# Two layers of two blocks on one core: the eight feature tiles of u_hi 1088 bytes apart instead of 1024

## The chip, the core and the metric

One Trainium2 chip, one of its cores. The metric is the device time of one execution in microseconds (us). Engine names: PE is TensorE (PEld its weight load), DVE is VectorE, ACT is ScalarE, POOL is GpSimd, SP issues the loads. "The stationary operand" is the one that a weight load puts into the array before a matmul, "the moving operand" the one that the matmul then streams through.

## What is computed

The reference runs two blocks of two layers over x [256 tokens, 1024 features]. The first block's layers are an attention (differential in layer 0, neighbourhood in layer 1), a SwiGLU feed-forward of width 2816 and a gated per-layer embedding. The second block's layers are a mixer (gated convolution and pooling in layer 0; a forgetting attention and a block attention in layer 1) and a convolutional feed-forward of width 2816. A root-mean-square norm stands ahead of each. Cut to what matters here:

```python
hn = rmsnorm(h, norm_mix[i]);  h = h + attention(hn)          # q, k, v and output products, 1024 wide
h = h + (silu(hn @ w_gate) * (hn @ w_up)) @ w_down             # 1024 -> 2 x 2816 -> 1024
h = h + sigmoid(hn @ ple_w_gate) * (p[i] @ ple_w_proj)         # 1024 -> 1024
h = h + (silu(conv(z[..., :2816])) * z[..., 2816:]) @ w_out    # second block's feed-forward
```

All arrays are float32. Nearly all the work is products of a [256, K] activation with a weight matrix that is read once from HBM.

## The kernel before

Activations lie with features on the 128 partitions: eight feature tiles (KT = 8) of 256 tokens (S = 256). A float32 product is made of three float32r matmuls: each operand is split exactly into a high and a low part, and the product is hi*hi + hi*lo + lo*hi (`mm3`, L198). Every matmul is issued at L195 by `mm`, so all products share that line in the profile and are told apart by their tiles.

`Weights` (L53 to L104) reads the weight chunks of 128 x 1024 float32 (4096 bytes on each partition) in the order in which PE takes them: SP loads a chunk into one of five `stage` buffers (L71), ACT writes `w_hi` (L88), DVE writes `w_lo` (L89), eight buffers of each. A block of 128 x 128 weights is a slice of 512 bytes on each partition.

The moving operand of a product is one of these:

- `u_hi`, `u_lo` (`split_act`, L221): the operand of eight feature tiles, two buffers each. ACT writes u_hi (L256, L572, L616, L885, L898), DVE u_lo (L258, L573, L617 and others). They are read by the input products `out_tile` into `ps_g` (all q, k, gate, up and in-products) and by the output products of the attentions and of the even mixer into `acc`. In the v-products (`ps_v`, `pz`) the parts change places: slices of u are stationary, and the weights move.
- `m` (L724): the high and the low part of one feed-forward tile, side by side in one tile of 2048 bytes, the moving operand of the down-products into `acc`. `pool_m` is built in the same way.
- `p_part`: the split embedding inputs, the high and the low part in two tiles, moving operands of `ps_p`.

For one pair of weight block and feature tile the order is: w_hi stationary with u_hi moving, w_hi again with u_lo, w_lo with u_hi. Each matmul has a weight load of its own, and the load for the next matmul runs while a matmul streams.

The tile pools place their buffers one behind the other in SBUF. The starts on a partition in the built program, and what each leaves over when divided by 512 (a weight block's length):

| tile | start before | left over | start after | left over |
|---|---|---|---|---|
| w_hi, w_lo (8 + 8 buffers) | 53216 + 4096 i | 480 | the same | 480 |
| u_hi, first buffer, tile k | 118752 + 1024 k | 480 | 118752 + 1088 k | 480 + 64 k |
| u_hi, second buffer, tile k | 126944 + 1024 k | 480 | 127392 + 1088 k | 416 + 64 k |
| u_lo, both buffers | 135136 + 1024 k | 480 | 136032 + 1024 k | 352 |
| p_part | 184288 | 480 | 185184 | 352 |
| m, pool_m | 192544 | 32 | 193440 | 416 |

So "the offset" of a moving operand to the weight blocks, the difference of the two remainders (counted round 512), was 0 for u_hi, u_lo and p_part and 64 for m. In the text a negative offset means that the moving operand's start lies below the weight block's in this count.

Of the kernel before, what the change touches and what calls it, by code (L numbers as in the profile page):

```python
# [11 lines left out]
F32R = mybir.dt.float32r  # L12
# [8 lines left out]
FF = 2816  # L21
FT = FF // 128
NEG = -1.0e30
FLOOR = -3.0e38
# [7 lines left out]

# After how many steps of the products around them the parts of an attention are issued.
LAG = {"da": (2, 8, 11, 14), "da_every": 3, "pair": (2, 5, 7), "every": 2}
# [16 lines left out]


class Weights:  # L53
    """The weights in the order in which TensorE takes them: loaded ahead, each split
    exactly into two float32r parts (w = hi + lo). A chunk with a destination is split
    into tiles that it makes."""

# [49 lines left out]
def network(ctx: ExitStack, tc: tile.TileContext, x_t, p_t, cols, b_v, na_bias, t5_bias, w_mats, out):  # L107
# [9 lines left out]

# [1 line left out]
    chunks = []  # L119
# [40 lines left out]

# [1 line left out]
    h = const.tile([128, KT, S], F32, name="h")  # L162
# [6 lines left out]

# [1 line left out]
    off = const.tile([128, S], F32, name="off")  # L171
# [30 lines left out]

# [1 line left out]
    clock = [0, 0]  # L204
# [16 lines left out]
    def split_act(tag="u"):  # L221
        hi = acts.tile([128, KT, S], F32R, tag=tag + "h", name="u_hi")
        lo = acts.tile([128, KT, S], F32R, tag=tag + "l", name="u_lo")
        return hi, lo

    # ---- RMSNorm: the gain goes into the next product's operand, the root mean square
    # into its result ----
    class Norm:
        pass

    def stats_bank(n, b, src, final=False):
        """Sums of squares by token; with final, of the features with the final gain."""
        if b == 0:
            sq = work.tile([128, 2, S], F32, tag="ssq", bufs=2, name="ssq")
        else:
            sq = work.tile([128, 2, S], F32, tag="sq", bufs=1, name="sq")
        if final:
            for i in range(2):
                nc.scalar.activation(sq[:, i, :], src[:, i, :], AF.Square, scale=col("norm_final", 2 * b + i))
        else:  # L240
            nc.scalar.activation(sq, src, AF.Square)
        if b == 0:
            setattr(n, "ssq2" if final else "ssq", sq)
        else:
            ssq = n.ssq2 if final else n.ssq
            if b == 3 and hasattr(n, "end"):
                n.end = sq
            else:
                nc.vector.tensor_add(ssq, ssq, sq)  # L249

    def norm_bank(n, b, src, gain):
        """Bank b (two feature tiles) of the next product's operand from src [128, 2, S]."""
        if b == 0:
            n.u = split_act()
        for i in range(2):
            nc.scalar.activation(n.u[0][:, 2 * b + i, :], src[:, i, :], AF.Copy, scale=gain(2 * b + i))  # L256
        for i in range(2):
            nc.vector.scalar_tensor_tensor(n.u[1][:, 2 * b + i, :], src[:, i, :], gain(2 * b + i),  # L258
                                           n.u[0][:, 2 * b + i, :].bitcast(F32),
                                           op0=OP.mult, op1=OP.subtract)  # L260

    def mean_square(ps, ssq, end=None):
        """end: the last bank's squares, where ssq is without them."""
        half = work.tile([128, S], F32, tag="on", bufs=2, name="half")
        nc.vector.tensor_add(half, ssq[:, 0, :], ssq[:, 1, :])
        for t in range(2):
            s = slice(t * 128, (t + 1) * 128)
            mm(ps[:, t:t + 1], half[:, s], ones, True, end is None)
            for i in range(0 if end is None else 2):
                mm(ps[:, t:t + 1], end[:, i, s], ones, False, i == 1)  # L270

    def rstd_a(n, eps=1e-6):
        ps = psum.tile([128, 4], F32, tag="m", bufs=2, name="ps_ss")
        two = hasattr(n, "ssq2")
        mean_square(ps[:, 0:2], n.ssq, getattr(n, "end", None))
        if two:
            mean_square(ps[:, 2:4], n.ssq2)
        st = work.tile([128, 8], F32, tag="rstd", name="rstd")
        n.rstd = st[:, 0:2]
        nc.vector.tensor_scalar(st[:, 2:4], ps[:, 0:2], 1.0 / D, eps, op0=OP.mult, op1=OP.add)  # L280
        nc.gpsimd.tensor_tensor(n.rstd, st[:, 2:4], mhalf, op=OP.pow)  # L281
        if two:
            # the mean square of what the first norm leaves, and both factors together
            nc.vector.tensor_mul(st[:, 4:6], n.rstd, n.rstd)
            nc.vector.scalar_tensor_tensor(st[:, 4:6], ps[:, 2:4], 1.0 / D, st[:, 4:6], op0=OP.mult, op1=OP.mult)
            nc.vector.tensor_scalar(st[:, 4:6], st[:, 4:6], eps, None, op0=OP.add)
            nc.gpsimd.tensor_tensor(st[:, 6:8], st[:, 4:6], mhalf, op=OP.pow)
            nc.vector.tensor_mul(st[:, 6:8], st[:, 6:8], n.rstd)
            n.both = st[:, 6:8]
        else:  # L290
            n.both = n.rstd

    def spread(v):
        """v [128, 2], by token, as a row on every partition."""
        ps = psum.tile([128, S], F32, tag="m", bufs=2, name="ps_r")
        for t in range(2):
            nc.tensor.transpose(ps[:, t * 128:(t + 1) * 128], v[:, t:t + 1].to_broadcast([128, 128]), ident)
        r = work.tile([128, S], F32, tag="R", name="R")
        nc.scalar.activation(r, ps, AF.Copy)
        return r  # L300
# [10 lines left out]

# [1 line left out]
    def out_tile(o, u, nk=KT, w=None):  # L313
        """One tile of 128 output features: o [128, S] += W-block^T u."""
        hi, lo = W.take(nk * 128) if w is None else w
# [12 lines left out]
    class Acc:  # L328
        """Products with all eight output tiles open, one k-tile after the other."""

# [39 lines left out]

# [1 line left out]
    def transposes(a, skip):  # L372
        """a [128 q, 2, 256 k] -> [128 k, (k-tile, q)] in one bank, without blocks that are zero."""
        w = 384 if skip else 512
# [28 lines left out]
    def softmax_pair(sc, ps, bias, widths):  # L403
        """Rows of exp(s - max) for two row blocks, unnormalized, and 1/sum."""
        st = work.tile([128, 8], F32, tag="st", bufs=4, name="st")
# [87 lines left out]

# [1 line left out]
    lam = const.tile([128, 4], F32, name="lam")  # L495
# [4 lines left out]
    def small_constants():  # L500
        # the differential attention's bias, -2^-(head + 1) |q - k|
        nc.vector.scalar_tensor_tensor(dist, dist, -1.0, dist, op0=OP.mult, op1=OP.max)
# [19 lines left out]

# [1 line left out]
    def da_steps(g, q, k, v, bias, o, emitted):  # L524
# [54 lines left out]

# [1 line left out]
    def pair_steps(g, q, k, v, bias_of, is_causal, o, emitted, later):  # L581
# [79 lines left out]

# [1 line left out]
    na_tiles = {}  # L663
# [16 lines left out]

# [1 line left out]
    extra = {}  # L682
# [31 lines left out]

# [1 line left out]
    def silu_times(m, g, other):  # L716
# [47 lines left out]

# [1 line left out]
    p_split = {}  # L766
# [29 lines left out]

# [1 line left out]
    n = Norm()  # L798
# [25 lines left out]

    # between the blocks: h becomes its norm; the product that follows starts from h
    # with both gains, and its result takes both root mean squares
    def scale_h():
# [7 lines left out]

    # even mixer
    y = split_act()
# [90 lines left out]

    # the last norm, with tokens on partitions
    hg = work.tile([128, KT, S], F32, tag="bias", name="hg")  # L930
# [34 lines left out]
def _feature_tiles(w, idx=None):  # L965
    """[K, N] -> [N/128, 128, (K/128) * 128]: a block for each tile of output features."""
    k, n = w.shape
    return w.reshape(k // 128, 128, n // 128, 128).transpose(2, 1, 0, 3).reshape(n // 128, 128, k)
# [7 lines left out]
def _qkv(w):  # L976
    """Per group of 256 columns: two tiles of q, two of k, and v's 256 columns in two halves of k."""
    q, k, v = (_feature_tiles(w[:, i * D:(i + 1) * D]) for i in range(2)) and \
# [12 lines left out]
def _per_partition(v):  # L991
    """[..., n * 128] -> [128, ... * n]"""
    return np.asarray(v).reshape(-1, 128).T
# [96 lines left out]
class _Listed:  # L1090
    """Blocks of several widths, read like an array of blocks."""

# [5 lines left out]
```

## Time and profile before

| | |
|---|---|
| timed runs | 1291.64, 1292.86, 1293.36 us; median 1292.86 |
| profiled execution | span 1291.7 us from first to last instruction; of its own device time only this span is shown |
| PE busy | 1271.1 us (98%), 10448 matmuls |
| DVE, ACT, POOL busy | 933.6 us (72%), 696.7 us (54%), 31.1 us (2%) |
| granted TensorE clock | 0.996 on average |

Matmuls overlap: a matmul's record lasts some 280 ns, but the next one starts 118 to 120 ns after it. What counts is therefore the distance from start to start, which one reads from the chain of waits: a piece "11.52 PE ps_g x96" is 96 matmuls in a row in 11.52 us, 120.0 ns each.

### The profile page before, as it was taken

Reading aid. Unit: us, or ns where it says so; the run is one execution under the profiler, and the core shown is the slowest. Engines: PE = TensorE matmul, PEld = TensorE weight load, DVE = VectorE, ACT = ScalarE, POOL = GpSimd, SP = SyncE. Lnnn points to the kernel's source line nnn. Section 1 sums busy time; section 2 is a strip of 40 time slices with the busy share of each in tenths; the row PEclk is TensorE's granted clock in tenths of the full one; section 3 lists DMA queues with packets and bytes.
Section 4 is the critical chain, followed back from the end, with each engine's and each line's share of the span. In section 5 each row is a group of like instructions: output and inputs, shape, how many; then the busy total and the mean of one; then the engine's idle time right before and its main releaser. Section 6 shows DMA issues by size and latency. Waiting matters only on the chain.

```text
span 1291.7 us, 25713 instructions
## 1 busy us (share of the span) xinstructions
PE 1271.1 (98%) x10448; PEld 1242.7 (96%) x10448; DVE 933.6 (72%) x1708; ACT 696.7 (54%) x1178; POOL 31.1 (2%) x54
## 2 busy tenths in 40 slices
PE   6999999999999999999999999999999999999997
PEld 6999999999999999999999999999999899999997
DVE  7876766666976667666678888777787766877774
ACT  6776544444666554444456455554456555544543
POOL 1011000000010000000000000000000000000000
PEclk9999999999999999999999999999999999999998
DMA  8465556554646536565546375555545333655530
GB/s 291 146 194 171 174 181 190 186 187 149 208 151 184 172 115 198 185 197 181 175 139 202 133 242 180 182 188 186 180 154 191 107 130 124 208 184 180 185 126 34
DMA packets 62936, 222.46 MB, mean 172 GB/s; under 512 B 7265, under 2 KB 7777, under 8 KB 62689
## 3 DMA queue, kind: packets, MB, share of 16 engines
q1 hardware_dynamic: 60768, 214.52, 50.6%
q0 software_dynamic: 1616, 5.77, 1.9%
q8 instruction: 82, 1.34, 0.4%
q10 hardware_dynamic: 432, 0.53, 0.1%
q14 instruction: 38, 0.30, 0.1%
HBM read 219.74 MB, written 1.05 MB: 171 GB/s over the span
## 4 chain that ended last, share of the span: by engine, by line
PE 91%; DVE 3%; issue 3%; DMA 1%; ACT 1%; POOL 1%; POOLq 0%; DVEq 0%; ACTq 0%; SPq 0%
PE ps_g L195 52%; PE acc L195 26%; PE ps_v L195 5%; PE ps_S L195 3%; PE ps_V L195 2%; PE ps_t L381 1%; DVE w_lo L89 1%; PE ps_p L195 1%; POOL rstd L281 1%; PE pz L195 0%; PE ps_ss L195 0%; DVE u_lo L258 0%; DMA stage<-w_ev_out 0%; DVE ssq L249 0%; DVE h L359 0%
## 5 line engine op out<-in xcount | busy, mean ns | idle before, releaser
L88 ACT ACTIVATE w_hi<-stage 128x1024 fp32r<-128x1024 f32 (+2 forms) x413 | 428.7, 1040 | 447.0 <-PE ps_g L195 176.2
L89 DVE TENSOR_TENSOR w_lo<-stage,w_hi 128x1024 fp32r<-128x1024 f32 (+2 forms) x413 | 495.9, 1202 | 218.9 <-ACT w_hi L88 218.0
L195 PE MATMUL ps_g<-u_hi,w_hi 128*128 128x256 f32 x2048 | 585.5, 287 | 7.4 <-ACT w_hi L88 7.1
L195 PE MATMUL ps_g<-u_hi,w_lo 128*128 128x256 f32 x2048 | 581.6, 284 | 1.0 <-DVE w_lo L89 1.0
L195 PE MATMUL ps_g<-u_lo,w_hi 128*128 128x256 f32 x2048 | 582.0, 285 | 0.4 <-DVE u_lo L258 0.4
L195 PEld LDWEIGHTS ps_g<-u_hi,w_hi 128*128 128x128 f32 x2048 | 393.2, 192 | 11.3 <-ACT w_hi L88 7.1
L195 PEld LDWEIGHTS ps_g<-u_hi,w_lo 128*128 128x128 f32 x2048 | 393.4, 192 | 1.5 <-DVE w_lo L89 1.2
L195 PEld LDWEIGHTS ps_g<-u_lo,w_hi 128*128 128x128 f32 x2048 | 393.7, 192 | 1.1 <-DVE u_lo L258 0.6
L195 PE MATMUL acc<-m,w_hi 128*128 128x256 f32 x1408 | 251.5, 280 | 0.0
L195 PEld LDWEIGHTS acc<-m,w_hi 128*128 128x128 f32 x1408 | 215.6, 188 | 0.3 <-DVE m L724 0.2
L195 PE MATMUL acc<-m,w_lo 128*128 128x256 f32 x704 | 196.7, 280 | 0.0
L195 PEld LDWEIGHTS acc<-m,w_lo 128*128 128x128 f32 x704 | 132.6, 188 | 0.0
L195 PE MATMUL acc<-u_hi,w_hi 128*128 128x256 f32 x256 | 73.6, 291 | 0.0
L195 PE MATMUL acc<-u_lo,w_hi 128*128 128x256 f32 x256 | 72.4, 284 | 0.3 <-DVE u_lo L573 0.3
L195 PE MATMUL acc<-u_hi,w_lo 128*128 128x256 f32 x256 | 72.2, 284 | 0.0
L411 ACT ACTIVATE sc<-sc,st 128x256 f32<-128x256 f32 (+1 forms) x96 | 46.0, 482 | 18.6 <-DVE st L409 18.5
L195 PE MATMUL ps_v<-w_hi,u_hi 128*128 128x256 f32 x176 | 52.2, 296 | 0.0
L195 PE MATMUL ps_v<-w_lo,u_hi 128*128 128x256 f32 x176 | 50.3, 286 | 0.0
L195 PE MATMUL ps_v<-w_hi,u_lo 128*128 128x256 f32 x176 | 50.3, 286 | 0.0
L195 PEld LDWEIGHTS acc<-u_hi,w_hi 128*128 128x128 f32 x256 | 48.8, 192 | 1.5 <-issue 0.6
L195 PEld LDWEIGHTS acc<-u_lo,w_hi 128*128 128x128 f32 x256 | 49.1, 192 | 0.5 <-DVE u_lo L573 0.5
L195 PEld LDWEIGHTS acc<-u_hi,w_lo 128*128 128x128 f32 x256 | 49.0, 192 | 0.0
(189 smaller groups left out, 1223.8 us busy)
## 6 DMA issues: line engine op xcount, KB each, us to landing
stage<-w_gu SPq DMA_DIRECT2D x88, 512.0 KB, 3.9
stage<-w_in SPq DMA_DIRECT2D x88, 512.0 KB, 3.4
stage<-w_down SPq DMA_DIRECT2D x44, 512.0 KB, 4.1
stage<-w_out SPq DMA_DIRECT2D x44, 512.0 KB, 3.4
stage<-w_na_qkv SPq DMA_DIRECT2D x24, 512.0 KB, 4.3
stage<-w_da_qkv SPq DMA_DIRECT2D x23, 512.0 KB, 4.4
stage<-w_od_in SPq DMA_DIRECT2D x22, 512.0 KB, 3.9
stage<-w_gate SPq DMA_DIRECT2D x16, 512.0 KB, 3.4
```

Source lines behind the costliest of these rows:

```text
L88: self.nc.scalar.activation(hi[:, s], t[:, s], AF.Copy)
L89: self.nc.vector.tensor_sub(lo[:, s], t[:, s], hi[:, s].bitcast(F32))
L195: nc.tensor.matmul(o, a, b, start=start, stop=stop, **kw)
L281: nc.gpsimd.tensor_tensor(n.rstd, st[:, 2:4], mhalf, op=OP.pow)
L381: nc.tensor.transpose(ps[:, o:o + 128], a[:, qt, kk * 128:(kk + 1) * 128], ident)
L411: nc.scalar.activation(sc[:, i, :widths[i]], sc[:, i, :widths[i]], AF.Exp, bias=st[:, 2 + i:3 + i], accum_out=st[:, 4 + i:5 + i])
```

## The change

`split_act` makes u_hi's tile 7 x 272 + 256 elements long instead of 8 x 256, and hands out an object whose index [:, k, a:b] gives the 256 elements from k x 272 on. Feature tile k of u_hi so starts 1088 k bytes into the tile. u_lo keeps its form. Since u_hi has two buffers, everything that the pools place behind it moves up by 896 bytes (2 x 448). Comments are taken out as well, so that line numbers differ (L195 is L210 in the changed kernel). The order of instructions on every engine and every semaphore wait are the same, instruction for instruction; only addresses differ, in 4992 matmuls and in the ACT and DVE instructions that write or read the tiles moved.

```diff
+PITCH = S + 16
...
+class Rows:
+    def __init__(self, t):
+        self.t = t
+
+    def __getitem__(self, at):
+        p, k, s = at
+        assert p == slice(None)
+        a, b = s.start or 0, S if s.stop is None else s.stop
+        return self.t[:, k * PITCH + a:k * PITCH + b]
...
     def split_act(tag="u"):
-        hi = acts.tile([128, KT, S], F32R, tag=tag + "h", name="u_hi")
+        hi = acts.tile([128, (KT - 1) * PITCH + S], F32R, tag=tag + "h", name="u_hi")
         lo = acts.tile([128, KT, S], F32R, tag=tag + "l", name="u_lo")
-        return hi, lo
+        return Rows(hi), lo
```

## Rows read from the trace of the kernel before

**Rows 1.** The page: busy time by engine, clock by slice, shares of the chain.
```profile
PE 1271.1 (98%) x10448; PEld 1242.7 (96%) x10448; DVE 933.6 (72%) x1708; ACT 696.7 (54%) x1178; POOL 31.1 (2%) x54
...
PEclk9999999999999999999999999999999999999998
...
PE 91%; DVE 3%; issue 3%; DMA 1%; ACT 1%; POOL 1%; POOLq 0%; DVEq 0%; ACTq 0%; SPq 0%
PE ps_g L195 52%; PE acc L195 26%; PE ps_v L195 5%; PE ps_S L195 3%; PE ps_V L195 2%; PE ps_t L381 1%; DVE w_lo L89 1%; PE ps_p L195 1%; POOL rstd L281 1%; PE pz L195 0%; PE ps_ss L195 0%; DVE u_lo L258 0%; DMA stage<-w_ev_out 0%; DVE ssq L249 0%; DVE h L359 0%
```
**Rows 2.** The chain, two feed-forwards: start us, us, engine, tile, line, count.
```profile
150.93 5.66 PE acc L195 x48
156.58 11.53 PE ps_g L195 x96
...
793.17 5.66 PE acc L195 x48
798.83 11.53 PE ps_g L195 x96
```
**Rows 3.** The chain, other products.
```profile
322.61 1.44 PE ps_p L195 x12
...
753.87 21.12 PE acc L195 x176
...
977.68 5.78 PE pz L195 x48
...
1029.23 1.44 PE ps_v L195 x12
```
**Rows 4.** The chain: transposes of 128 moving columns, one with its neighbours.
```profile
1027.47 0.33 PE ps_t L381 x3
1027.80 1.43 PE ps_g L195 x12
```
**Rows 5.** Groups of instructions: line, engine, tiles, shape, count, busy us, mean ns, idle.
```profile
L195 PE MATMUL ps_g<-u_hi,w_hi 128*128 128x256 f32 x2048 | 585.5, 287 | 7.4 <-ACT w_hi L88 7.1
L195 PE MATMUL ps_g<-u_hi,w_lo 128*128 128x256 f32 x2048 | 581.6, 284 | 1.0 <-DVE w_lo L89 1.0
L195 PE MATMUL ps_g<-u_lo,w_hi 128*128 128x256 f32 x2048 | 582.0, 285 | 0.4 <-DVE u_lo L258 0.4
...
L195 PE MATMUL acc<-m,w_hi 128*128 128x256 f32 x1408 | 251.5, 280 | 0.0
...
L195 PE MATMUL acc<-m,w_lo 128*128 128x256 f32 x704 | 196.7, 280 | 0.0
L195 PE MATMUL acc<-u_hi,w_hi 128*128 128x256 f32 x256 | 73.6, 291 | 0.0
...
L195 PE MATMUL ps_v<-w_hi,u_hi 128*128 128x256 f32 x176 | 52.2, 296 | 0.0
```
**Rows 6.** Windows in those feed-forwards: us, busy (count) by engine, clock, DMA share, GB/s.
```profile
157.00:168.00 11.00, 11.00 (x94) 11.00 (x93) 6.70 (x8) 4.40 (x6) 0.00 (x0) 1.00 0.58 190
799.00:810.00 11.00, 11.00 (x94) 11.00 (x93) 7.21 (x11) 5.14 (x7) 0.00 (x0) 1.00 0.61 203
151.00:156.50 5.50, 5.50 (x49) 5.50 (x48) 4.21 (x6) 2.57 (x4) 0.00 (x0) 1.00 0.61 201
793.30:798.80 5.50, 5.50 (x49) 5.50 (x49) 5.38 (x11) 3.14 (x6) 0.00 (x0) 1.00 0.67 223
```
**Rows 7.** Waits of PE over the span: who waited for whom, us, times, longest.
```profile
PE ps_g L195 <- ACT w_hi L88: 7.1, 1, 7.1
PE ps_r L297 <- POOL rstd L281: 3.4, 4, 2.5
PE ps_r L297 <- DVE rstd L288: 1.3, 1, 1.3
PE ps_g L195 <- DVE w_lo L89: 1.0, 1, 1.0
```

## The prediction

> **What bounds the kernel now.** I read the page first [rows 1]: PE is busy 98% of the span, and PE's work is 91% of the chain that ended last. The granted clock reads nine tenths or more (its upper level, 2.4 GHz) in every slice but the last. PE hardly waits for anyone: its longest waits add up to some 13 us, 7.1 of them a single wait at the start [rows 7]. So the time is the number of matmuls times the distance from one start to the next, and that distance is what a change of addresses can touch. The records' own lengths (280 to 296 ns in [rows 5]) overlap and do not give it; the chain does, which shows stretches of matmuls in a row. Here the reader should divide:
>
> - products with u moving into ps_g: 11.53 us for 96, 120.1 ns each [rows 2];
> - down-products with m moving into acc: 5.66 us for 48, 117.9 ns each [rows 2];
> - the even mixer's output product, u moving into acc: 21.12 us for 176, 120.0 ns; the embedding product, p_part moving: 1.44 for 12, 120 ns; v-products, weights moving over slices of u: 1.44 for 12, 120 ns [rows 3];
> - transposes, 128 columns moving instead of 256: 0.33 us for 3, 110 ns [rows 4].
>
> All but the transposes have the same shape (128 rows, 128 columns, 256 moving columns), so the 2.2 ns between 117.9 and 120.1 need a cause. It is not the output: u into acc runs at 120.0, m into acc at 117.9. It is not that the moving tile stays the same over eight blocks of weights, which holds for both of these. It is not the work beside it: the two feed-forwards of [rows 2] have different DVE and ACT work (in 11 us 6.70 against 7.21 us of DVE, 4.40 against 5.14 of ACT; in 5.5 us of down-product 4.21 against 5.38 of DVE, [rows 6]) and the same 11.53 and 5.66. What goes with the number in all five kinds is the offset between the moving operand and the weight blocks, from the table of starts: 0 where the row says 120, 64 bytes where it says 117.9. My reading is that the weight load and the stream that runs beside it get into each other's way in SBUF when they start at the same remainder, and somewhat less at 64 bytes. That is an inference from one pair of offsets.
>
> The Trainium skill speaks against it and against any effect of this change: "TensorE: Matmul & The Clock Gate", section "Part 2: What happens when you issue a matmul", says that loading the next tile's weights doesn't take SBUF read bandwidth from the running matmul, since the two come through independent ports. By that rule every distance stays and the sum below is 0. The trace does not agree so far as the offset is the cause of the 2.2 ns; if something else is, rule and trace go together. It is rival B.
>
> **The change, part by part.** It removes, adds and moves no instruction and no wait; order and semaphores are the same on all engines and queues. The writers of u_hi (ACT) write the same 256 elements for each tile, so they cost the same; if they didn't, PE runs on anyway, since DVE stands idle 4.30 and ACT 6.60 of 11 us there [rows 6]. Loads go to the stage buffers, which don't move. I cost all this at 0. What is left are new offsets for four operands. Counts from [rows 5]: u into ps_g 3 x 2048, u into acc 3 x 256, u in ps_v 3 x 176, and 48 of pz [rows 3], of which two thirds involve u_hi: 4992, and one third u_lo: 2496. m has 1408 + 704 = 2112.
>
> 1. u_hi, 4992 matmuls. Over its eight tiles the offset takes each of 0, 64, ... 448 once, in the first buffer; in the second the same eight values turned round by one. Counted round 512, one tile in eight stays at 0 and keeps 120.1. Two in eight lie 64 away (64 and 448, which is -64): I give them m's 117.9, 2.2 ns less. Five in eight have offsets that no row shows. The nearest rows are 117.9 and 120.1, and I take the middle, 1.1 ns less. Mean: (2 x 2.2 + 5 x 1.1) / 8 = 1.24 ns.
> 2. u_lo, 2496 matmuls, goes from 0 to -128: not shown either, the middle, 1.1 ns less.
> 3. m, 2112 matmuls, goes from +64 to -64, through the 896 bytes that the longer tiles push it on. Same distance, other side: I take no change.
> 4. p_part (12 in 1.44 us, 1% of the chain) goes to -128: under 0.2 us, left out.
>
> The sum: of ps_g's 6144 x 120.1 ns = 738 us, 52% x 1291.7 = 672 us stand on the chain [rows 1], a share of 0.91; elsewhere PE has slack and a shorter distance is lost. ps_g: (4096 x 1.24 + 2048 x 1.1) x 0.91 = 6.7 us. The rest of u: 896 x 1.24 + 448 x 1.1 = 1.6 us. Together 8.3 us. Against the span of 1291.7 this gives 1283.4. The median of the runs shown lies 1.2 us above that span, which I add: **1284.5 us**. What is late next if PE quickens: a ps_g block of 24 matmuls would take some 30 ns less of 2.88 us. ACT and DVE have the room named above and DMA engines are busy 0.58 to 0.67 there [rows 6], so no new wait takes it back.
>
> Bounds for the unseen offsets. Below, the nearest row is the transposes' 110 ns [rows 4], where each stream is half as long: 10 ns less at most. All 3120 unseen u_hi matmuls and all of u_lo there would save 5616 x 10 ns = 56 us, far from any row with 256 columns; I keep a part of it (rival D). Above, no stretch of whole-array matmuls runs slower than 120.1; but that is the value at the one offset where both start together, and a worse one isn't excluded. I allow as much above 120.1 as m lies below: 122.3.
>
> The same skill page, section "Back-to-back issue gap", puts the distance of 256 columns alone at N / 2.4 + 2.5, an estimate of 109 ns. The 110 ns of the transposes agree with a floor near it. By it all plain products here hold some 9 to 11 ns that something other than streaming costs.
>
> **The rivals.**
>
> - **B, no effect: 1292.9 us.** The 2.2 ns come from something else that sets m apart, above all that its high and low part lie side by side in one tile (p_part's and u's do not), or only distances finer than 64 bytes count. Then all offsets run as before. Against it: in m's triples the stream repeats the same part and changes part exactly as u's do, and pz, whose moving slices start 1056 bytes apart, takes 5.78 us for 48 or 120.4 ns [rows 3], although it streams 264 columns where the others stream 256; so addresses seem to matter there too. For it: only one offset besides 0 is known.
> - **C, slower: 1302 us.** The sign of the offset decides. A stream reads 1024 bytes while the load reads 512, so a stream that starts ahead (m's +64) stays ahead, and one that starts behind must pass the load in mid-stream. The change puts m at -64 and u_lo at -128. Price: m back to 120.1, 2112 x 2.2 = 4.6 us; u_lo to 122.3, 2496 x 2.2 = 5.5 us; u_hi has as many offsets ahead as behind, 0. Together 10.1, times the 0.91 about 9.3 us. It decides from the point on where m's distance rises by more than about 2 ns with u_hi's mean unmoved.
> - **D, deep gain: 1259 us.** Streams that start further than 64 bytes apart hardly meet. The unseen offsets go to the middle between 117.9 and 110, 114, that is 6.1 ns less: (3120 + 2496) x 6.1 = 34 us, and the two tiles of u_hi at 64 add 1248 x 2.2 = 2.7; times 0.91, 33.6 us. For it: 9 to 10 ns stand between the plain products and the transposes. Against it: 64 bytes recovered only 2.2 of them.
>
> **How the numbers follow.** The forecast (some of the u products quicker, m about as it was) has a chance of 0.49, rival B 0.15, C 0.19, D 0.17. The forecast's own range is 1272 to 1290: half again the gain that all of u at 117.9 would give (6864 x 2.2 x 0.91 = 14 us), down to a third of mine. A difference of 0.2%, 2.6 us, is about what a measurement of this kernel can tell from none. Faster by more than that: the forecast but for its end nearest to no change (0.47) and D, 0.64. Slower: C, 0.19. Within: B and that end, 0.17. The range reaches up to C's time, 1302, and down to 1262, just short of D's: beyond are the dearer half of C and some half of D, under 2 in 10.
>
> **What would show it.** The counts, the order and the granted clock stay. In the chain, 96 in ps_g read 11.53 now; the forecast gives 11.42 (64 x 1.24 + 32 x 1.1 = 115 ns less), B 11.53, C 11.6, D about 11.1. The 48 of the down-product read 5.66: forecast, B and D 5.66, C 5.77. The wrong step would be the first or second if ps_g's stretches stay at 11.53, the third if the down-product moves. If both stretches shorten as forecast and the span does not, the share on the chain was wrong, and waits of PE for w_hi or w_lo would show it.

## The result and the profile after

The changed kernel takes 1275.97 us (median of four runs, 1273.52 to 1278.36) against 1292.48 (four runs, 1291.64 to 1293.36): a ratio of 0.9871, 95% interval 0.9856 to 0.9885, or 16.5 us less. The profiled execution took 1276.78 us with a span of 1275.0; the span of before was 1291.7. The forecast was 1284.5: the direction is right, the gain is twice the one forecast.

The page after, busy time, clock by slice, shares of the chain [rows 1]:

```profile
PE 1253.7 (98%) x10448; PEld 1223.2 (96%) x10448; DVE 933.0 (73%) x1708; ACT 697.3 (55%) x1178; POOL 31.2 (2%) x54
...
PEclk9999999999999999999999999999999999999998
...
PE 87%; DVE 5%; issue 3%; ACT 2%; POOL 1%; DMA 1%; POOLq 0%; DVEq 0%; ACTq 0%; SPq 0%
```

Counts, clock and the busy time of DVE and ACT are those of before. PE's busy time is 17.4 us less: the whole difference lies in how closely its matmuls follow each other. More matmuls have new addresses than the 4992 that involve u_hi: u_lo's 2496 and m's 2112 are pushed on as well, as the table of starts has it.

The kernel has four feed-forwards: the first block's for layers 0 and 1 (here from about 150 and 492 us) and the second block's for layers 0 and 1 (from about 783 and 1095 us). [rows 2] show the first and the third. The chain after, in the first, at the start of the second, and in the third (start us, us, engine, tile, line, count):

```profile
149.83 5.46 PE acc L210 x48
155.29 11.31 PE ps_g L210 x96
166.60 5.45 PE acc L210 x48
...
492.38 5.65 PE acc L210 x48
498.03 11.25 PE ps_g L210 x96
...
783.06 5.46 PE acc L210 x48
788.52 11.31 PE ps_g L210 x96
799.83 5.52 PE acc L210 x48
...
816.66 5.58 PE acc L210 x48
...
833.55 5.66 PE acc L210 x48
...
850.51 5.66 PE acc L210 x48
```

Two things are to be read here. The input products take 11.31 us for 96, 117.8 ns each, where [rows 2] had 11.53 and 120.1; in the second and fourth feed-forwards they take 11.25, 117.2 ns each. And the down-products, which were at 5.66 us (117.9 ns) in the kernel before, take 5.46 (113.7 ns) in the first feed-forward and at the start of the third, and are back at 5.66 from 833 us on. In the second they take 5.65 throughout; in the fourth 5.53 to 5.65.

Summing the distances from each matmul's start to the next over the whole span (worked out from the trace's records, by the tile written) gives where the 16.5 us come from: ps_g 757.5 us before and 745.8 after (-11.7), acc with m moving 249.8 and 246.3 (-3.5), acc with u moving 96.1 and 94.8 (-1.3); every other tile differs by at most 0.5.

**Why the down-products of the third feed-forward lose their gain again.** The timeline of the changed kernel around the middle of the stretch that starts at 833.55, where the m of the stretch's second feed-forward tile comes in (start us, us, engine, line, operation):

```profile
835.66 0.30 PEld L210 LDWEIGHTS acc<-m,w_hi 128*128 128x128 f32 x2
835.75 0.42 DVE L739 TENSOR_TENSOR m<-t,m 128x256 fp32r<-128x256 f32 x1
835.77 0.39 PE L210 MATMUL acc<-m,w_hi 128*128 128x256 f32 x2
...
836.00 0.41 PEld L210 LDWEIGHTS acc<-m,w_hi 128*128 128x128 f32 x2
...
836.12 0.50 PE L210 MATMUL acc<-m,w_hi 128*128 128x256 f32 x2
...
836.45 0.28 PE L210 MATMUL acc<-m,w_lo 128*128 128x256 f32 x1
...
836.80 0.28 PE L210 MATMUL acc<-m,w_lo 128*128 128x256 f32 x1
...
837.16 0.28 PE L210 MATMUL acc<-m,w_lo 128*128 128x256 f32 x1
```

DVE writes m's low part from 835.75 to 836.17. PE's second matmul on this m was due at 836.23 and starts at 836.34: the pair takes 0.50 us instead of 0.39, so PE waited 0.11 us. In the kernel before the same write ended 0.17 us ahead of its use (at 847.32; the first of the pair starts at 847.37, the second 0.12 later):

```profile
846.90 0.42 DVE L724 TENSOR_TENSOR m<-t,m 128x256 fp32r<-128x256 f32 x1
...
847.37 0.40 PE L195 MATMUL acc<-m,w_hi 128*128 128x256 f32 x2
```

The quicker PE has thus caught up with the engine that feeds it, by a small amount each time: with m moving, 28 distances in the trace after are over 135 ns (6.1 us in all), 11 before (2.4 us). Sixteen of the 28 are this wait, in the middle of eight down-products each of the third and the fourth feed-forward; one of the 11 is.

The wait can have an after-effect: ahead of the one shown, seven triples (the three matmuls of one weight block and its part of m) take 2.38 us (113.3 ns a matmul), behind it, from the three w_lo rows above on, seven take 2.47 (117.6), with the same operands at the same offset. But it does not always: behind eight of the sixteen waits the distance stays near 117.8, behind the other eight it is back at 113.3 after a few matmuls. Nor is it the only way to the longer distance: in the second feed-forward every down-product runs at 117.8 from its start, with no such wait in it. Two distances at one offset is what the prediction had not thought of; the experiments come back to it.

### The profile page after: what moved, and what is told of

The parts are those of the page before. It is cut to its first block, busy times and chain, and to the rows that moved or that the text cites. A ratio compares the mean times of both kernels' runs of the same rounds, so it can differ in the third digit from the quotient of the medians.

```text
span 1275.0 us, 25713 instructions
## 1 busy us (share of the span) xinstructions
PE 1253.7 (98%) x10448; PEld 1223.2 (96%) x10448; DVE 933.0 (73%) x1708; ACT 697.3 (55%) x1178; POOL 31.2 (2%) x54
## 4 chain that ended last, share of the span: by engine, by line
PE 87%; DVE 5%; issue 3%; ACT 2%; POOL 1%; DMA 1%; POOLq 0%; DVEq 0%; ACTq 0%; SPq 0%
PE ps_g L210 50%; PE acc L210 24%; PE ps_v L210 5%; PE ps_S L210 3%; DVE w_lo L104 2%; PE ps_V L210 2%; PE ps_t L396 1%; ACT w_hi L103 1%; ACT u_hi L271 1%; DVE u_lo L273 1%; POOL rstd L296 1%; DVE ssq L264 1%; PE pz L210 0%; DVE h L374 0%; PE ps_p L210 0%
## 5 line engine op out<-in xcount | busy, mean ns | idle before, releaser
L210 PE MATMUL ps_g<-u_hi,w_hi 128*128 128x256 f32 x2048 | 578.7, 283 | 8.0 <-ACT w_hi L103 7.0
L210 PE MATMUL ps_g<-u_lo,w_hi 128*128 128x256 f32 x2048 | 577.6, 282 | 0.4 <-DVE u_lo L273 0.4
L210 PE MATMUL ps_g<-u_hi,w_lo 128*128 128x256 f32 x2048 | 574.1, 281 | 0.9 <-DVE w_lo L104 0.9
L210 PEld LDWEIGHTS ps_g<-u_hi,w_hi 128*128 128x128 f32 x2048 | 384.7, 188 | 12.6 <-ACT w_hi L103 7.0
L210 PEld LDWEIGHTS ps_g<-u_lo,w_hi 128*128 128x128 f32 x2048 | 386.4, 189 | 1.3 <-DVE u_lo L273 0.6
L210 PEld LDWEIGHTS ps_g<-u_hi,w_lo 128*128 128x128 f32 x2048 | 386.2, 189 | 1.5 <-DVE w_lo L104 1.2
L210 PE MATMUL acc<-m,w_hi 128*128 128x256 f32 x1408 | 247.8, 280 | 0.1
L210 PEld LDWEIGHTS acc<-m,w_hi 128*128 128x128 f32 x1408 | 214.8, 188 | 0.8 <-ACT m L738 0.2
L210 PE MATMUL acc<-m,w_lo 128*128 128x256 f32 x704 | 195.7, 278 | 0.0
L210 PEld LDWEIGHTS acc<-m,w_lo 128*128 128x128 f32 x704 | 133.0, 189 | 0.0
L210 PE MATMUL acc<-u_hi,w_hi 128*128 128x256 f32 x256 | 72.8, 288 | 0.0
L210 PE MATMUL acc<-u_lo,w_hi 128*128 128x256 f32 x256 | 71.8, 282 | 0.3 <-DVE u_lo L588 0.3
L210 PE MATMUL acc<-u_hi,w_lo 128*128 128x256 f32 x256 | 71.5, 281 | 0.0
L210 PE MATMUL ps_v<-w_hi,u_hi 128*128 128x256 f32 x176 | 51.9, 295 | 0.0
L210 PE MATMUL ps_v<-w_lo,u_hi 128*128 128x256 f32 x176 | 50.1, 285 | 0.0
L210 PE MATMUL ps_v<-w_hi,u_lo 128*128 128x256 f32 x176 | 49.8, 283 | 0.0
L210 PEld LDWEIGHTS acc<-u_hi,w_hi 128*128 128x128 f32 x256 | 48.0, 189 | 1.5 <-issue 0.6
L210 PEld LDWEIGHTS acc<-u_lo,w_hi 128*128 128x128 f32 x256 | 48.2, 188 | 0.5 <-DVE u_lo L588 0.5
L210 PEld LDWEIGHTS acc<-u_hi,w_lo 128*128 128x128 f32 x256 | 48.1, 188 | 0.0
```

The lines of the kernel that those rows point to most:

```text
L210: nc.tensor.matmul(o, a, b, start=start, stop=stop, **kw)
```

## The experiments

Theory A: the offset between moving operand and weight blocks sets the distance, whatever made it so. Its rivals: the uneven distance of the tiles does it, by itself; the place in SBUF does it, and not the offset; and, on how it adds up, that each matmul has the distance of its own offset. But for the second, the kernels below differ from the kernel before only in pads: tile pools that are opened ahead of another pool and push it on, each with one memset of its own on POOL. In two of them u_lo gets a pool of its own besides.

### Shift without the pitch (e1_shift_only)

u_hi's tiles stay 1024 bytes apart; u_lo gets a pool of its own with a pad of 896 bytes ahead. So u_hi stays at offset 0, u_lo is at -128 and m at -64, as in the changed kernel.

```diff
+    pad2 = ctx.enter_context(tc.tile_pool(name="pad2", bufs=1))
+    pad2_t = pad2.tile([128, 224], F32, name="pad2_t")
+    nc.gpsimd.memset(pad2_t, 0.0)
+    acts_lo = ctx.enter_context(tc.tile_pool(name="acts_lo", bufs=2))
...
-        lo = acts.tile([128, KT, S], F32R, tag=tag + "l", name="u_lo")
+        lo = acts_lo.tile([128, KT, S], F32R, tag=tag + "l", name="u_lo")
```

> u_hi keeps its pitch of 1024 bytes; a pad of 896 bytes between u_hi and u_lo gives u_lo, p_part and m the places that the change gives them (offsets to the weight blocks: u_hi 0, u_lo -128, m -64). Theory 1, the offset of moving operand and weight block sets the distance from start to start: the 48 of the down-product fall from 5.66 us to 5.45 as with the change, the 96 of ps_g stay between 11.31 and 11.53 (only u_lo's third is off 0), total 1283 to 1288 us. Theory 2, it is the uneven pitch of u_hi that does it, places alone do nothing: all as before, 1292 us.

Measured: 1274.95 us, ratio 0.9862 (0.9848 to 0.9877). The chain:

```profile
148.41 5.65 PE acc L199 x48
154.07 11.20 PE ps_g L199 x96
...
831.72 5.57 PE acc L199 x48
837.29 11.31 PE ps_g L199 x96
```

The shift alone gives as much as the change. u_hi itself has not moved, and yet 96 input products take 11.20 us, 116.7 ns each, in the first feed-forward; 22 of the 32 stretches of 96 take 11.30 or 11.31, 117.8 ns each, as in the second pair of rows. m, at the same -64 as in the changed kernel, takes 5.65 in the first feed-forward where that took 5.46, and 5.44 in the second where that takes 5.65.

### Pitch without the shift (e2_pitch_only)

The changed kernel with u_hi's tile 64 bytes longer, so that its second buffer and all that lies behind move by whole multiples of 512: u_lo at 0, m at +64, as before. Room for it comes from the forget gate's `lf`, which is put into a tile that is already there.

```diff
-        hi = acts.tile([128, (KT - 1) * PITCH + S], F32R, tag=tag + "h", name="u_hi")
+        hi = acts.tile([128, (KT - 1) * PITCH + S + 16], F32R, tag=tag + "h", name="u_hi")
...
-        lf = work.tile([128, 2, 8], F32, tag="lf", bufs=1, name="lf")
-        nc.vector.tensor_sub(lf.rearrange("p a b -> p (a b)"), t[:, 2, :], t[:, 1, :])
+        nc.vector.tensor_sub(t[:, 0, :], t[:, 2, :], t[:, 1, :])
+        lf = t[:, 0, :].rearrange("p (a b) -> p a b", a=2)
```

> u_hi at a pitch of 1088 bytes, but its tile made 64 bytes longer so that everything behind it moves by 1024 bytes and keeps its offset (u_lo and p_part 0, m +64). Theory 1: the down-product stays at 5.66 us for 48; the 96 of ps_g fall, to some 11.35, total about 1281 us. Theory 2: ps_g as with the change, 11.31, down-product too as the uneven pitch has changed the rhythm of PE as a whole: 1276 us.

Measured: 1281.23 us, ratio 0.991 (0.9896 to 0.9925).

```profile
149.50 5.66 PE acc L210 x48
155.16 11.32 PE ps_g L210 x96
```

m is where it was and keeps 5.66. The pitch gives 0.9% by itself, the shift 1.4%, both together 1.3%. Summed over the span as above, ps_g's distances give 11.1 us here, 12.4 in e1 and 11.7 in the changed kernel, m's give nothing here, 3.9 in e1 and 3.5 in the changed kernel: pitch and shift are two ways to much the same gain in ps_g, and only the shift moves m.

### Everything at -64, even pitch (e3_all_m64)

448 bytes ahead of the u buffers and 448 ahead of the pool that holds m: u_hi, u_lo and m all at -64, tiles 1024 apart.

```diff
+    pad1 = ctx.enter_context(tc.tile_pool(name="pad1", bufs=1))
+    pad1_t = pad1.tile([128, 112], F32, name="pad1_t")
+    nc.gpsimd.memset(pad1_t, 0.0)
     acts = ctx.enter_context(tc.tile_pool(name="acts", bufs=2))
+    pad3 = ctx.enter_context(tc.tile_pool(name="pad3", bufs=1))
+    pad3_t = pad3.tile([128, 112], F32, name="pad3_t")
+    nc.gpsimd.memset(pad3_t, 0.0)
```

> pitch 1024 everywhere, two pads of 448 bytes put u_hi, u_lo and m all at the one constant offset of -64 bytes. Theory 1: u runs like m did with the change at -64, 113.5 ns from start to start: 96 of ps_g in 10.9 us, total about 1250 us, faster than the change. Theory 2 (a constant offset locks, an uneven one doesn't): ps_g at 11.5, total 1288 to 1292.

Measured: 1252.74 us (1252.23, 1252.34, 1253.13 and one run at 1261.65), ratio 0.9714 (0.9678 to 0.9751). This beats both kernels, by 40 us the one before.

```profile
147.88 5.44 PE acc L201 x48
153.32 10.88 PE ps_g L201 x96
...
784.50 5.53 PE acc L201 x48
790.03 10.88 PE ps_g L201 x96
800.91 5.59 PE acc L201 x48
```

10.88 us for 96 and 5.44 for 48 are 113.3 ns each, for u and m alike. In the third feed-forward a down-product takes 0.09 to 0.15 us more: the trace has the same wait for m there, a distance of up to 0.22 us in its middle, and here the matmuls behind it go back to 113.3. By the prediction's formula ps_g alone would give 6144 x (120.1 - 113.3) x 0.91 = 38.0 us; summed from the trace it gives 31.1, m 6.4 and u into acc 3.3. A new wait shows that the cover gets thin, PE's waits over the span:

```profile
PE ps_g L201 <- ACT u_hi L262: 1.2, 3, 0.6
```

That was 0.3 us, twice, in the changed kernel, and not among the waits of before [rows 7].

### The place, not the offset (e4_abs64)

64 bytes ahead of the weights' buffers: weights, u and m all move by 64 and keep their offsets.

```diff
+    pad0 = ctx.enter_context(tc.tile_pool(name="pad0", bufs=1))
+    pad0_t = pad0.tile([128, 16], F32, name="pad0_t")
+    nc.gpsimd.memset(pad0_t, 0.0)
     split = ctx.enter_context(tc.tile_pool(name="split", bufs=N_HI))
```

> a pad of 64 bytes ahead of the weights moves weights, u and m together: every absolute place changes by 64, no offset between them does. If only the offset of moving operand to weight block counts: as before, 1292 us, 11.53 and 5.66. If the absolute place counts: the 120 and 118 ns change by 1 ns or more.

Measured: 1291.70 us, ratio 0.9994 (0.9985 to 1.0003), and the stretches of before:

```profile
149.35 5.66 PE acc L198 x48
155.01 11.52 PE ps_g L198 x96
```

Moving everything does nothing; moving the operands against the weights does. With the third experiment this settles that the offset is the cause. One reading of it remains, that the operands meet ACT's and DVE's writes into the weight buffers and not the weight loads. The traces speak against it (ps_g in the four feed-forwards, distances up to 126 ns): while neither engine writes w_hi or w_lo, the distances average 119.9 ns in the kernel before (323 of them) and 113.4 in e3 (239), while both write, 120.0 and 113.4.

### The other offsets (e5_all_128, e5_all_256, e5_all_384, e5_all_480, e6_all_64, e6_all_192, e6_all_416)

The edit of e3 with the first pad at 128, 256, 384, 480, 64, 192 and 416 bytes in place of 448: u_hi, u_lo and m all at that offset (384 is -128, 480 is -32, 416 is -96). e6_all_192 has four runs, the others one each.

```diff
-    pad1_t = pad1.tile([128, 112], F32, name="pad1_t")
+    pad1_t = pad1.tile([128, 32], F32, name="pad1_t")
```

> pitch 1024 everywhere, u_hi, u_lo and m all at the one constant offset of +128 bytes to the weight blocks. Theory A, only the separation counts and 64 bytes below is as good as any: 113.5 ns from start to start as at -64 (96 of ps_g in 10.9 us), total 1253 us. Theory B, the side counts (rival C with its sign turned: a stream that starts ahead of the load loses, one that starts behind gains): as at +64, 117.9 ns, 96 in 11.3 us, total 1278 us or more.

> the same with the constant offset of 256 bytes, half way round. Theory A: 113.5 ns or less, 1253 us or less. Theory B: between +128 and -64, 10.9 to 11.5 us for 96, total 1253 to 1290 us.

> the same with the constant offset of -128 bytes. Theory A: 1253 us. Theory B: 113.5 ns or less, down to the transposes' 110: 96 in 10.6 to 10.9 us, total 1230 to 1253 us.

> the same with the constant offset of -32 bytes. Theory A: part of the way from 120 to 113.5, 96 in 11.0 to 11.4 us, total 1258 to 1280 us. Theory B: the same as A here, or already as at -64, 1253 us.

> constant offset of +64 bytes for u_hi, u_lo and m. If the side counts: 117.9 ns as m showed at +64 in the kernel before, 96 of ps_g in 11.3 us, 48 of m in 5.66, total some 1280 us. If 117.9 was only what the stretch ahead of m (u at 120) left it with: 113.5 ns for all, 96 in 10.9 us, total 1253 us.

> constant offset of +192 bytes. If distances repeat every 256 bytes, as 0 and 256 (120 ns both) and +128 and -128 (118.7 both) say: the same as -64, 113.5 ns, 96 in 10.9 us, total 1253 us. If -64 is good because the stream starts just below the weight block: 117 to 120 ns, 1275 to 1293 us.

> constant offset of -96 bytes, between -64 (113.5 ns) and -128 (118.7). A narrow place at -64: 117 to 119 ns, total 1275 to 1290 us, as -32 gave 118.3 and 1282.7. A wide one reaching down from -64: 113.5 ns, 1253 us.

Measured, with the chain's stretches of 96 in ps_g, 32 in each execution (us, and ns for each matmul):

| offset of all | time us | kernel before, same chip | 96 in ps_g | ns |
|---|---|---|---|---|
| 0 (before, m at +64) | 1292.48 | | 11.53 | 120.1 |
| 256 | 1295.64 | 1293.99 | 11.52 | 120.0 |
| 128 | 1288.61 | 1293.99 | 11.39 | 118.7 |
| -128 | 1288.01 | 1293.99 | 11.39 | 118.7 |
| -96 | 1286.28 | 1292.53 | 11.39 in 29, 11.26 to 11.27 in 3 | 118.7, 117.3 |
| -32 | 1282.71 | 1293.99 | 11.36 | 118.3 |
| 64 | 1278.10 | 1292.53 | 11.31 in 30, 10.88 in 2 | 117.8, 113.3 |
| 192 | 1258.36 (0.9741, 0.9696 to 0.9785) | 1292.53 | 10.88 in 22, 11.31 in 10 | 113.3, 117.8 |
| -64 (e3) | 1252.74 (0.9714, 0.9678 to 0.9751) | 1292.91 | 10.88 | 113.3 |

The chain at +128:

```profile
150.50 5.70 PE acc L201 x48
156.19 11.39 PE ps_g L201 x96
```

at -128:

```profile
156.07 11.39 PE ps_g L201 x96
```

at 256:

```profile
149.57 5.76 PE acc L201 x48
155.33 11.52 PE ps_g L201 x96
```

At each of these offsets the 48 of m take half of the 96 of u in the first feed-forward, so u and m do not differ but by their offset. 256 is as slow as 0, +128 as -128, and 192 shows the same two rates as 64: as far as it was tried, the pattern repeats with 256 bytes, not with the weight block's 512. The changed kernel's trace has that period inside its stretches, where each of u_hi's eight tiles starts 64 bytes further on against the weights: the three matmuls of a tile average, from tile to tile, 118.3, 116.8, 118.3 and 118.0 ns, then again 118.3, 116.4, 118.3 and 118.0 (first feed-forward).

The offsets 64 and 192 have the two rates within one execution. The chain at +64, third feed-forward:

```profile
823.98 11.31 PE ps_g L201 x96
835.29 5.55 PE acc L201 x48
840.84 10.88 PE ps_g L201 x96
851.72 5.65 PE acc L201 x48
857.38 11.31 PE ps_g L201 x96
```

and at +192:

```profile
779.78 10.88 PE ps_g L201 x96
790.66 5.61 PE acc L201 x48
796.27 11.31 PE ps_g L201 x96
807.58 5.58 PE acc L201 x48
813.16 10.88 PE ps_g L201 x96
```

The rate changes inside a down-product (5.55 to 5.61 is neither 5.44 nor 5.65) and the next input product goes on at the rate that it ends with. So the distance has a memory: it is carried from stretch to stretch until something disturbs it. That need not show as a wait: at +64 the change inside the down-product at 835.29 comes with no distance above 119 ns around it. At +192 all of the second feed-forward runs at the longer distance. Which of the two a run falls into, and when, differs: the four runs at +192 took 1253.10 to 1265.58 us, and one run at -64 took 9 us more than the other three. That these spreads are the two rates was not shown, since only one execution of each was profiled.

### Does each matmul have the distance of its own offset? (e7_hi_m64_lo_0)

u_hi and m at -64, u_lo at 0 (pads of 448 ahead of u_hi, 64 ahead of u_lo, which has a pool of its own as in e1, 384 ahead of m's pool).

```diff
+    pad1_t = pad1.tile([128, 112], F32, name="pad1_t")
...
+    pad2_t = pad2.tile([128, 16], F32, name="pad2_t")
...
+    acts_lo = ctx.enter_context(tc.tile_pool(name="acts_lo", bufs=2))
...
+    pad3_t = pad3.tile([128, 96], F32, name="pad3_t")
```

> u_hi at a constant offset of -64, u_lo at 0, m at -64, pitch 1024. If each matmul has the distance of its own offset: a third at 120, two thirds at 113.4, 115.6 ns on average, 96 of ps_g in 11.10 us, total about 1262 us. If it is the sequence that counts, as the kernel with u_hi at 0 and u_lo at -128 says (11.20 to 11.31 us, less than the 11.52 and 11.39 that either offset gives alone): another number, between 10.88 and 11.52.

Measured: 1280.87 us in one run (before: 1292.53). The chain:

```profile
150.25 5.44 PE acc L205 x48
155.70 11.45 PE ps_g L205 x96
167.15 5.45 PE acc L205 x48
...
807.49 11.30 PE ps_g L205 x96
...
824.37 11.45 PE ps_g L205 x96
```

m has the short distance, 113.3 ns, as in e3. The input products do not: if two of three matmuls took 113.3 and the third 120.0, 96 would take 64 x 113.3 + 32 x 120.0 = 11.09 us; with 117.8 for the two, 11.38. 25 of the 32 stretches take 11.45, more than either; the other seven take 11.30 or 11.31. In e1 it was the other way about: 64 x 120.0 + 32 x 118.7 = 11.48 expected from the table, 11.20 and 11.31 measured. The distance belongs to the sequence of offsets, not to the single matmul. Theory A holds as to the cause, and falls as to how it adds up.

## Why the prediction was right and wrong

**Right: what bounds the kernel, and by what it can change.** The chain of waits, divided by its counts, found a difference of 2.2 ns between products of one shape, and the table of starts its cause. e4 (offsets kept, 0.9994) and e3 (offsets changed, 0.9714) show it. The time follows the distance: no new instruction, no other clock, and PE's waits over the span nearly those of [rows 7]. What failed is the size of two terms, ps_g (6.7 us against 11.7) and m (0 against 3.5), and the rule that each matmul has the distance of its own offset, by which they were worked out.

**Wrong in size, steps 1 and 2: the unseen offsets at "the middle, 1.1 ns less" and the tile that "stays at 0 and keeps 120.1".** ps_g went from 120.1 to 117.8 ns in the first and third feed-forwards and to 117.2 in the second and fourth, 2.3 to 2.9 ns where I had 1.24 for u_hi and 1.1 for u_lo. The unmoved tile has its part in it: no tile's three matmuls average more than 118.3 ns in the first feed-forward. The term of ps_g was 6.7 us and measured 11.7. Summing offset by offset with the table of the experiments would give a stretch of 11.39 us, with four of u_hi's eight tiles at 117.8, two at 118.7, two at 120.0, and u_lo at 118.7, or 11.24 with the four at 113.3. 11.31 and 11.25 were measured, which lie between, but e1 and e7 show that such a sum does not hold.

The share on the chain, 0.91, was too high: the 3891 matmuls of ps_g in stretches of 96 and more give 9.2 us, 2.4 ns each, the other 2253, in short pieces between other work, 2.5 us, 1.1 ns each. With 2.4 ns for all, 14.7 us, the share that came through is 0.80; in e3, 31.1 of 6144 x 6.8 = 41.8 us, it is 0.74. The other products of u, 1.6 us in the sum, gave 1.3 in acc and nothing sure in the v-products.

**Wrong, step 3: "Same distance, other side: I take no change" for m.** The term of 0 measured 3.5 us. The 117.9 ns of [rows 2] was one of two rates that an offset of 64 allows, and the row showed only the one that the kernel before happened to run at. After the change m runs at 113.7 for the first feed-forward, at 117.8 for the second, and at both in the third and fourth. Had it stayed at 113.7 everywhere, 2112 x 4.2 = 8.9 us would have come of it. Of the 5.4 that did not come, the second feed-forward holds some 2.2 (528 x 4.2, an estimate), without a wait; the rest lies with the late m, and with what follows it, in the third and fourth.

The three terms as measured, 11.7, 1.3 and 3.5, make up the 16.5 us where the prediction's made 8.3. That the direction came out is not luck, since the offset is the cause; that 117.9 ns is the distance of an offset of 64 was read from a single row, and did not hold.

**Wrong: "no new wait takes it back".** I had looked at idle time of DVE and ACT in windows of 11 us [rows 6], where there is room. The wait that came is for one 0.42 us write of DVE whose lead on its reader shrank from 0.17 to 0.06 us (836.17 to 836.23), and that was too little.

**The rivals.** B, no effect, is refuted by the result and by e1 to e3. The Trainium skill, "TensorE: Matmul & The Clock Gate", section "Part 2: What happens when you issue a matmul", has weight load and stream come through independent ports. The traces do not agree with what the prediction drew from it, that every distance stays: the distance went from 120.1 to 113.3 ns with the operands' place against the weights. Whether it is the two reads that meet was not shown. C, slower through the sign, is refuted: apart from its waits m was never slower at -64 than at +64, and +128 and -128 are alike (11.39). D's depth is there (113.3, near its 114 at the unseen offsets) but not where D put it: 118.7 at 128, 120.0 at 256. Its time, 1259, was reached at +192 (1258.36) and passed at -64 (1252.74), not by this change. The prediction estimated 109 ns for 256 columns alone from the same page of the Trainium skill, section "Back-to-back issue gap". No stretch shown here comes to it; 113.3 is the shortest. The transposes' 110 ns, which the prediction reads as agreeing, are for 128 columns and say nothing of 256.

**Still open.** What in SBUF or PE makes the distance depend on the offset, what rule turns a sequence of unlike offsets into one distance, and what picks one of the two rates at odd multiples of 64: m at -64 runs at 113.3 in the first feed-forward and at 117.8 in the second in the changed kernel, and the other way round in e1. That the reads of weight load and stream meet in one bank or port with a period of 256 bytes would fit, but was only argued. Other orders of the three matmuls, and m moved without u, were not tried.

## What to carry to other kernels

Where PE is the bound and every matmul has a weight load of its own, divide the chain's stretches by their counts, and if products of one shape differ, look at the starts of the moving operands and the weights. A pad of some hundred bytes ahead of a pool is a cheap trial: here 896 bytes in two pads gave 2.9%, more than the uneven pitch. Try several offsets and measure each; one row's distance is not the distance of its offset, and a mixture is not its mean.

## What the runs showed of the hardware

- Matmuls of 128 x 128 x 256 in float32r with a weight load each start 113.3 to 120.1 ns apart, at a granted clock of 0.996 to 0.998 over the span (the 2.4 GHz level), and what was changed between the runs is the offset of moving operand to weights. The offsets tried fit a pattern that repeats every 256 bytes: slowest at 0 and 256 (120.0 to 120.1), 118.3 to 118.7 at -32, 128 and -128 and in 29 of 32 stretches at -96.
- At 64, 192 and -64 there are two distances, 117.8 and 113.3, each of which can last for many stretches. Behind eight of sixteen waits of PE of up to 0.11 us, for m at -64, the longer one followed; it also changes without a wait.
- Alternating offsets can be quicker than each of them alone (u_hi at 0 and u_lo at -128: 116.7 or 117.8) or slower than their mean (u_hi at -64 and u_lo at 0: 119.3 in 25 of 32 stretches).
